# A decoder step on one core: the pairs' elementwise steps and the token sums on VectorE alone, sums begun at the normed prompt, half of the embedding's products later

## The chip, the cores and the metric

The kernel runs as one program on one core of a Trainium2 chip. The metric is the device time of one execution in microseconds (us), as the median of several runs. A profile of one further execution comes with it. Its engines are TensorE (PE, with its weight loads PEld), VectorE (DVE), ScalarE (ACT), GpSimd (POOL) and SyncE (SP, which issues most transfers). The engines run side by side, each in the order of its own queue, and wait for one another by semaphores.

## The reference, cut to what matters

One layer of a hybrid decoder, for a prompt of 512 tokens and for 8 samples of 4 tokens with 4,096 cached positions each; all 544 tokens go through the same weights. After the token mixers it computes, per token:

```
x   = layer_norm(ALPHA * x + mixed, ln1_g, ln1_b)
gate, up = split(x @ w_ffn_up, 2)                 # 1024 -> 2 x 2816
ffn = (silu(gate) * up) @ w_ffn_down
ple = sigmoid(x @ w_ple_gate) * (p @ w_ple)       # p: 256 per token
x   = layer_norm(ALPHA * x + ffn + ple, ln2_g, ln2_b)
```

The change lies between the first of these norms and the product with w_ffn_down. `p @ w_ple` is called the embedding below.

## The kernel before, in words

**Layout.** Activations stand transposed: 128 channels of a block on the partitions, tokens along the free axis (columns 0 to 511 the prompt, 512 to 543 the samples). Full precision is had from three products of parts: a matrix is split into a high part (a copy rounded to the matmul's type) and a low part (the matrix minus its high part), and high x high, high x low and low x high are added up in PSUM (`passes`, L464). The high part is a ScalarE activation or a VectorE copy, the low part an elementwise subtraction (`split`, L275). In the profile wh and wl are a weight unit's parts, x1h and x1l those of the normed x, h of the FFN's hidden rows, th and tl those of the token sums.

**Weights** come in units of 128 x 1024 (512 KB), numbered in the order of use: `GN` (L32) lists the groups and their lengths, `FA` (L29) the units of the first four FFN columns, among which the two units of the embedding stand as "wp". `SRC` (L39) gives each unit's place in memory. `loader` (L372) and `splitter` (L388) fetch and split them ahead of the products.

**The order of the work.** One Python program writes out every engine's queue by hand. `Weave` (L64) plays streams (generators) against a model of the engines' clocks: `wv.t` is TensorE's time, `wv.act`, `wv.dve` and `wv.pool` those of the others; a stream yields a time, a condition or a flag, and the stream of the best priority that may go on goes on. So costs and conditions in the planner decide in which order an engine's instructions stand; the hardware then follows that order and waits where the model was off. Two helpers choose an engine: `tt` (L262) gives a two-input step to GpSimd where the model lets GpSimd finish 0.3 us before VectorE, `evac` (L268) chooses between VectorE and ScalarE. As every instruction is recorded by the engine's wrapper, nearly all VectorE, ScalarE and GpSimd work bears L146, and products L238; the tile names tell them apart.

**From the first norm on.** `norms1` (L1073) norms the prompt in two halves of 256 columns; `norm1` (L1049) scales the residual tiles rr in place, and per group of two channel blocks writes the high part with the bias on ScalarE and the low part with the bias on VectorE. The samples' 32 columns come by a stream of their own, `sample_tail` (L966), which waits for the decode attention, makes its projections and its norm in the tile res, and writes the sample columns of x1h and x1l (L1040). Flags ("x1", part, group) tell what is ready.

**The first four FFN columns** (`NA` = 4, L1421 to L1446) are plain products in two token parts: columns 0 to 255 as soon as the first prompt half is normed, then columns 256 to 543 once the second half and the samples are. In the first part `embed` (L1319) puts four of the embedding's eight output blocks in front of column 1 and four in front of column 2; its results wait in the tiles pw.

**The other 18 FFN columns and the gate of the embedding** go in 22 pairs (`pair`, L497): two weight units and the two token halves are combined as in a 2 x 2 block product with seven instead of eight multiplications. `pair_splits` (L402) forms the four combinations of the weights (s1 = c + d, c = a - c, a = s1 - a, b = b - a; c lies in the tile wq, a and b in wr, s1 in ws) and splits seven operands. `token_sums` (L1375) forms the four combinations of the tokens once, from xw = x1h + x1l, as the tiles tw, and splits them; the flag "tok" lets the pairs begin (L1448). `combine` (L534) adds the seven results up on VectorE, and `act` (L1455, L1490) applies the gate. Behind the 22 pairs `h_parts` (L1475) splits the hidden rows and the products with w_ffn_down begin, two output blocks at a time in the order in which hidden rows come.

**Room.** Large tiles share 39 slots (`slot`, L199); split weights have four buffers of each part.

Of the kernel before, what the change touches and what calls it, by code (L numbers as in the profile page):

```python
# [20 lines left out]
NT = 544  # L21
# [6 lines left out]
EMB = (1, 2)  # L28
FA = []  # L29
for _c in range(NA):  # L30
    FA += [("wp", _w) for _w in range(2) if EMB[_w] == _c] + [("up", 2 * _c), ("up", 2 * _c + 1)]
GN = [("in", 20), ("ga", 8), ("gc", 8), ("ap", 4), ("cp", 4), ("wo", 8), ("wo2", 6),  # L32
      ("fa", len(FA)), ("fb", 2 * NA), ("up", 44 - 2 * NA), ("pg", 8), ("dn", 22)]
# [8 lines left out]
SRC += [BASE["wo2"] + len(FA) + _i for _i in range(NU - BASE["up"])]  # L42
# [133 lines left out]
def step_kernel(ctx: ExitStack, tc: tile.TileContext, xT, pT, ck, cvv, state, pt, W, cv, cc, yT, kT, vT, cvo):  # L176
# [98 lines left out]
    def split(hi, lo, src, *then):  # L275
# [7 lines left out]
        def low():  # L283
            (tt if near else V.tensor_tensor)(out=lo, in0=src, in1=hi.bitcast(F32), op=ALU.subtract)
            flag.update(then)
# [116 lines left out]
    def pair_splits(n):  # L402
# [3 lines left out]
        def put(i, src):  # L406
            sop[n, i] = [big.tile([128, 512], F32R, tag=x, bufs=4, name=x) for x in ("wh", "wl")]
            cur["w"] += 1
            split(*sop[n, i], src, ("so", n, i))
# [14 lines left out]
        tt(out=s1, in0=c, in1=d, op=ALU.add)  # L424
        tt(out=c, in0=a, in1=c, op=ALU.subtract)
        yield done(("so", n, 0))
        tt(out=a, in0=s1, in1=a, op=ALU.subtract)
# [8 lines left out]
        tt(out=b, in0=b, in1=a, op=ALU.subtract)  # L436
# [60 lines left out]
    def pair(n, out):  # L497
# [6 lines left out]
        for i in range(7):  # L504
# [12 lines left out]
            for k in range(4):  # L517
# [3 lines left out]
                for l, (a, b) in enumerate(((w[0], y[0]), (w[0], y[1]), (w[1], y[0]))):  # L521
                    mm(HT * 4.25e-4, o, a[:, c], b, k == 0 and l == 0, k == 3 and l == 2)
# [443 lines left out]
    def sample_tail():  # L966
# [71 lines left out]
        for i, op in ((L1G, ALU.mult), (L1B, ALU.add)):  # L1038
            V.tensor_tensor(out=res, in0=res, in1=cvt[:, i:i + 8].unsqueeze(2).to_broadcast([128, 8, 32]), op=op)
        for g in range(4):  # L1040
# [5 lines left out]
    x1, x1p = [], []  # L1046
    tot1 = []

    def norm1(s, c0, c1, after, tag):  # L1049
# [3 lines left out]
        def each(g):  # L1053
# [8 lines left out]
            for e in range(2):  # L1062
                S.activation(out=h[:, e, c0:c1], in_=x[:, e], func=AF.Identity, bias=bs[e])

            def low():
                for e in range(2):
                    V.scalar_tensor_tensor(out=lo[:, e, c0:c1], in0=x[:, e], scalar=bs[e],
                                           in1=h[:, e, c0:c1].bitcast(F32), op0=ALU.add, op1=ALU.subtract)
                flag.add(("x1", s, g))
            wv.when(on(h), low)  # L1070
        yield from norm(xs, 1.0, c1 - c0, tag, norm_room(), tot1[0][:, c0:c1], each, L1G)

    def norms1():  # L1073
# [4 lines left out]
        rr.clear()  # L1078
# [37 lines left out]
    def main():  # L1116
# [202 lines left out]
        def embed(n, base):  # L1319
            for c in range(len(pw), n):  # L1320
# [4 lines left out]
                                    base + 8 * FA.index(("wp", c // 4)) + 2 * (c % 4))  # L1325
# [49 lines left out]
        def token_sums():  # L1375
            yield lambda: all(("x1", i, g) in flag for i in range(3) for g in range(4))
            x, sums = [], []
            for g in range(4):
                h, lo = (y.bitcast(F32) for y in x1p[g])
                x.append(slot("xw"))  # L1380
                yield pace
                tt(out=x[g], in0=h, in1=lo, op=ALU.add)
            h = lo = None
            for s in range(4):
                sums.append(slot("tw", (128, 4, HT)))
                for g in range(2):
                    l, r = (slice(0, HT), slice(HT, NT))
                    one = x[g + 2 * (s > 0)][:, :, l if s == 3 else r]
                    two = sums[s - 2 if s == 2 else 2][:, 2 * g:2 * g + 2] if s > 1 else x[g][:, :, r if s else l]
                    yield pace  # L1390
                    yield on(one, two)
                    tt(out=sums[s][:, 2 * g:2 * g + 2], in0=one, in1=two, op=ALU.subtract)
                one = two = None
            x.clear()
            for s in (1, 2, 0, 3):
                h, lo = (slot(y, (128, 4, HT), dt=F32R) for y in ("th", "tl"))
                for g in range(2):
                    c = slice(2 * g, 2 * g + 2)
                    yield pace
                    split(h[:, c], lo[:, c], sums[s][:, c], ("ts", s, g))  # L1400
# [14 lines left out]
        def pace():  # L1415
            return wv.dve < wv.t + 1.5
# [4 lines left out]
        for s, (c0, c1) in enumerate(((0, HA), (HA, NT))):  # L1421
            if s:
                ph.clear()
# [23 lines left out]
        p = t = None  # L1447
        yield done("tok")  # L1448
        n = 0
        for c in range(NA, 22):  # L1450
# [4 lines left out]
            def act(x, t, c, n):  # L1455
# [7 lines left out]
                tt(out=g, in0=g, in1=halves(r), op=ALU.mult)  # L1463
# [326 lines left out]
```

## Time and profile before

| | |
|---|---|
| median of 3 runs | 1031.42 us (1030.90 to 1032.55) |
| the profiled execution | 1026.15 us, its span 1024.4 us |
| busy share of the span | TensorE 93%, VectorE 78%, ScalarE 52%, GpSimd 23% |
| granted TensorE clock | 0.98 on average |
| moved | 222 MB, 217 GB/s on average |
| chain that ended last | TensorE 56%, VectorE 27%, DMA 6%, issue 5% |

The page gives the busy time of each engine, the span in 40 slices, the chain of work that ended last, and the costliest groups of instructions. A group or an instruction reads: line, engine, operation, tile written <- tiles read, partitions x elements and type; then the count and the busy time. "[1.40 <-POOL wq L146]" behind an instruction is the time for which its engine was idle before it, and what ended that. In a busy-time row by stretch each engine has its busy time and, in brackets, its instructions. TensorE's products overlap, so the distance between starts tells more of them than their durations.

### The profile page before, as it was taken

What the parts mean: (1) busy time and instruction counts of PE and PEld (TensorE: products, weight loads), DVE (VectorE), ACT (ScalarE), POOL (GpSimd) and SP (SyncE); (2) the same over time, 40 slices, a digit from 0 to 9 for tenths busy, and PEclk for the clock granted to TensorE, in tenths of its full rate; (3) what the DMA queues carried; (4) which work ended last, traced back from release to release, by engine and by line L of the source; (5) the groups of instructions that cost most, each with busy time, mean ns of one, the idle gap of its engine ahead of it and who ended that gap; (6) DMA issues with size and microseconds to landing.
All of it is one profiled execution on the core that took longest, in us unless ns stands there. A gap on an engine that the chain in (4) does not pass through costs nothing.

```text
span 1024.4 us, 22472 instructions
## 1 busy us (share of the span) xinstructions
PE 954.6 (93%) x7978; PEld 827.2 (81%) x7978; DVE 801.8 (78%) x1245; ACT 534.4 (52%) x1040; POOL 233.9 (23%) x202
## 2 busy tenths in 40 slices
PE   7989999999899999999999769999999999999994
PEld 5866667677777986787787769999999998999993
DVE  4798999999857466574986888899999999953375
ACT  4635666567785974343665444444434445621225
POOL 1320322224112002233322550212111112400021
PEclk9999999999999999999999979999999999999998
DMA  9959998999889999999999233322222221222302
GB/s 357 333 165 333 326 315 292 318 334 336 292 305 317 341 346 334 348 339 332 322 324 358 83 103 134 114 83 83 95 112 83 83 98 48 103 83 83 124 1 88
DMA packets 101378, 222.00 MB, mean 217 GB/s; under 512 B 11153, under 2 KB 14482, under 8 KB 101266
## 3 DMA queue, kind: packets, MB, share of 16 engines
q1 hardware_dynamic: 99394, 217.46, 60.6%
q10 hardware_dynamic: 1872, 3.11, 0.8%
q8 instruction: 63, 1.03, 0.4%
q14 instruction: 49, 0.40, 0.1%
HBM read 215.45 MB, written 5.07 MB: 215 GB/s over the span
## 4 chain that ended last, share of the span: by engine, by line
PE 56%; DVE 27%; DMA 6%; issue 5%; ACT 3%; SPq 2%; POOL 1%; ACTq 0%; DVEq 0%; POOLq 0%
PE g L238 38%; PE z L238 6%; PE av L238 6%; DVE wl L146 5%; DVE c L146 4%; DMA kv<-in_ck 2%; PE o L238 2%; DVE pw L146 2%; DVE x L146 2%; DVE pb L146 2%; DVE sg L146 2%; PE tp L238 2%; PE tp L243 1%; DVE wr L146 1%; SPq L228 1%
## 5 line engine op out<-in xcount | busy, mean ns | idle before, releaser
L146 ACT ACTIVATE wh<-wr 128x512 fp32r<-128x512 f32 x236 | 146.5, 626 | 238.8 <-PE g L238 102.0
L146 DVE TENSOR_TENSOR wl<-wr,wh 128x512 fp32r<-128x512 f32 x187 | 130.0, 701 | 50.3 <-ACT wh L146 49.7
L146 POOL TENSOR_TENSOR wl<-wr,wh 128x512 fp32r<-128x512 f32 x53 | 81.8, 1546 | 247.7 <-ACT wh L146 197.3
L238 PE MATMUL g<-xh,wh 128*128 128x272 f32 (+1 forms) x512 | 127.8, 321 | 6.1 <-ACT wh L146 6.1
L238 PE MATMUL g<-h,wh 128*128 128x272 f32 x704 | 123.1, 290 | 1.6 <-DVE h L146 1.6
L238 PE MATMUL g<-xl,wh 128*128 128x272 f32 (+1 forms) x512 | 119.9, 305 | 0.0
L238 PE MATMUL g<-xh,wl 128*128 128x272 f32 (+1 forms) x512 | 119.7, 305 | 0.2 <-POOL wl L146 0.2
L146 DVE SCALAR_TENSOR_TENSOR c<-u,cvt,c 128x512 f32<-128x512 f32 x120 | 109.2, 910 | 3.3
L238 PEld LDWEIGHTS g<-h,wh 128*128 128x128 f32 x704 | 103.2, 189 | 2.7 <-DVE h L146 2.3
L238 PEld LDWEIGHTS g<-xh,wh 128*128 128x128 f32 x512 | 83.2, 191 | 27.0 <-issue 17.5
L238 PEld LDWEIGHTS g<-xh,wl 128*128 128x128 f32 x512 | 83.6, 192 | 4.1 <-POOL wl L146 0.8
L238 PEld LDWEIGHTS g<-xl,wh 128*128 128x128 f32 x512 | 83.7, 191 | 2.6 <-DVE xl L146 0.5
L238 PE MATMUL g<-h,wl 128*128 128x272 f32 x352 | 80.0, 289 | 0.0
L238 PE MATMUL g<-x1h,wh 128*128 128x272 f32 (+2 forms) x216 | 66.1, 306 | 13.8 <-DVE sg L146 12.3
L238 PE MATMUL g<-x1h,wl 128*128 128x272 f32 (+2 forms) x216 | 66.4, 308 | 9.5 <-DVE wl L146 9.2
L238 PE MATMUL z<-kv,qblk 128*32 128x256 f32 x1024 | 65.0, 382 | 2.2 <-DMA kv<-in_ck 2.1
L146 ACT ACTIVATE wh<-wq 128x512 fp32r<-128x512 f32 x87 | 53.8, 620 | 23.4 <-PE g L238 17.9
L146 DVE TENSOR_TENSOR wl<-wq,wh 128x512 fp32r<-128x512 f32 x75 | 56.5, 758 | 10.9 <-ACT wh L146 10.4
L238 PE MATMUL g<-x1l,wh 128*128 128x272 f32 (+2 forms) x216 | 64.7, 299 | 0.0
L238 PE MATMUL av<-kv,dp 128*32 128x512 f32 x512 | 63.6, 613 | 0.0
L146 POOL TENSOR_TENSOR wl<-ws,wh 128x512 fp32r<-128x512 f32 x20 | 26.8, 1341 | 158.1 <-PE g L238 124.1
L146 ACT ACTIVATE pa<-pa 128x384 f32<-128x384 f32 (+1 forms) x96 | 52.5, 555 | 16.8 <-DVE pa L146 15.3
(319 smaller groups left out, 2455.8 us busy)
## 6 DMA issues: line engine op xcount, KB each, us to landing
kv<-in_ck SPq DMA_DIRECT2D x256, 256.0 KB, 4.5
kv<-in_cvv SPq DMA_DIRECT2D x256, 256.0 KB, 5.3
wr<-in_W SPq DMA_DIRECT2D x98, 512.0 KB, 4.3
wq<-in_W SPq DMA_DIRECT2D x37, 512.0 KB, 5.4
wa<-in_W SPq DMA_DIRECT2D x12, 512.0 KB, 9.9
xr<-in_xT SPq DMA_DIRECT2D x8, 272.0 KB, 5.2
out_yT<-pw SPq DMA_DIRECT2D x7, 272.0 KB, 2.3
out_kT<-qk ACTq DMA_DIRECT2D x4, 272.0 KB, 6.0
```

The costliest lines, as they stand in the source:

```text
L146: fn(**kw)
L228: eng.dma_start(out=out, in_=in_)
L238: T.matmul(out, lhsT=lhsT, rhs=rhs, start=start, stop=stop)
L243: T.transpose(out, in_, ident)
```

## The change

Six things change together.

1. `split` takes an engine for the low part; with it, the low part is not given to GpSimd. The pairs' weights, the token sums, the hidden rows and the normed prompt use it; the plain weights do not. The pairs' combinations and the products in `act` are written for VectorE instead of `tt`.
2. In `norm1` the bias is added in place, so that rr holds the normed x, and the parts come from an ordinary `split`.
3. `token_sums` no longer forms xw. It takes its prompt columns from rr as soon as the second prompt half is ready, 240 columns to a half, and the samples' 32 columns later from the tile res, which `sample_tail` hands over in `late_x`; rr is released there.
4. The token sums are split in the order 2, 1, 0, 3, and `pace` lets them go on only while VectorE's clock is less than 0.7 us (before 1.5) ahead of TensorE's.
5. Only the embedding's first unit stays among the first four columns (in front of column 1). The second has a group of its own behind them, and its four output blocks are computed behind the second token part, in front of the wait for "tok".
6. The planner's price of a pair's product is 0.126 us instead of 272 x 4.25e-4 = 0.116 us.

```diff
-EMB = (1, 2)
+EMB = (1,)
...
-      ("fa", len(FA)), ("fb", 2 * NA), ("up", 44 - 2 * NA), ("pg", 8), ("dn", 22)]
+      ("fa", len(FA)), ("fb", 2 * NA), ("wp", 1), ("up", 44 - 2 * NA), ("pg", 8), ("dn", 22)]
...
-    def split(hi, lo, src, *then):
+    def split(hi, lo, src, *then, eng=None):
...
-            (tt if near else V.tensor_tensor)(out=lo, in0=src, in1=hi.bitcast(F32), op=ALU.subtract)
+            (tt if near and eng is None else V.tensor_tensor)(out=lo, in0=src, in1=hi.bitcast(F32), op=ALU.subtract)
...
-            split(*sop[n, i], src, ("so", n, i))
+            split(*sop[n, i], src, ("so", n, i), eng=V)
...
-        tt(out=s1, in0=c, in1=d, op=ALU.add)
-        tt(out=c, in0=a, in1=c, op=ALU.subtract)
+        V.tensor_tensor(out=s1, in0=c, in1=d, op=ALU.add)
+        V.tensor_tensor(out=c, in0=a, in1=c, op=ALU.subtract)
         yield done(("so", n, 0))
-        tt(out=a, in0=s1, in1=a, op=ALU.subtract)
+        V.tensor_tensor(out=a, in0=s1, in1=a, op=ALU.subtract)
...
-        tt(out=b, in0=b, in1=a, op=ALU.subtract)
+        V.tensor_tensor(out=b, in0=b, in1=a, op=ALU.subtract)
...
-                    mm(HT * 4.25e-4, o, a[:, c], b, k == 0 and l == 0, k == 3 and l == 2)
+                    mm(0.126, o, a[:, c], b, k == 0 and l == 0, k == 3 and l == 2)
...
+        late_x.append(res)
         for g in range(4):
             yield lambda: len(x1p) > g
...
             for e in range(2):
-                S.activation(out=h[:, e, c0:c1], in_=x[:, e], func=AF.Identity, bias=bs[e])
-
-            def low():
-                for e in range(2):
-                    V.scalar_tensor_tensor(out=lo[:, e, c0:c1], in0=x[:, e], scalar=bs[e],
-                                           in1=h[:, e, c0:c1].bitcast(F32), op0=ALU.add, op1=ALU.subtract)
-                flag.add(("x1", s, g))
-            wv.when(on(h), low)
+                S.activation(out=x[:, e], in_=x[:, e], func=AF.Identity, bias=bs[e])
+            split(h[:, :, c0:c1], lo[:, :, c0:c1], x, ("x1", s, g), eng=V)
...
         def token_sums():
-            yield lambda: all(("x1", i, g) in flag for i in range(3) for g in range(4))
-            x, sums = [], []
-            for g in range(4):
-                h, lo = (y.bitcast(F32) for y in x1p[g])
-                x.append(slot("xw"))
-                yield pace
-                tt(out=x[g], in0=h, in1=lo, op=ALU.add)
-            h = lo = None
+
+            sums = []
+            yield lambda: all(("x1", 1, g) in flag for g in range(4))
             for s in range(4):
                 sums.append(slot("tw", (128, 4, HT)))
                 for g in range(2):
-                    l, r = (slice(0, HT), slice(HT, NT))
-                    one = x[g + 2 * (s > 0)][:, :, l if s == 3 else r]
-                    two = sums[s - 2 if s == 2 else 2][:, 2 * g:2 * g + 2] if s > 1 else x[g][:, :, r if s else l]
+                    d = sums[s][:, 2 * g:2 * g + 2, :240]
+                    one = rr[g + 2 * (s > 0)][:, :, 0:240] if s == 3 else rr[g + 2 * (s > 0)][:, :, HT:512]
+                    two = rr[g][:, :, HT:512] if s else rr[g][:, :, 0:240]
+                    if s > 1:
+                        two = sums[s - 2 if s == 2 else 2][:, 2 * g:2 * g + 2, :240]
                     yield pace
                     yield on(one, two)
-                    tt(out=sums[s][:, 2 * g:2 * g + 2], in0=one, in1=two, op=ALU.subtract)
-                one = two = None
-            x.clear()
-            for s in (1, 2, 0, 3):
+                    V.tensor_tensor(out=d, in0=one, in1=two, op=ALU.subtract)
+            yield lambda: all(("x1", 2, g) in flag for g in range(4))
+            res = late_x.pop()
+            yield on(res)
+            t1, t3, t2, t4 = (t[:, :, 240:] for t in sums)
+            for g in range(2):
+                c = slice(2 * g, 2 * g + 2)
+                V.tensor_tensor(out=t1[:, c], in0=res[:, c], in1=rr[g][:, :, 240:HT], op=ALU.subtract)
+            V.tensor_tensor(out=t3, in0=res[:, 4:8], in1=res[:, 0:4], op=ALU.subtract)
+            V.tensor_tensor(out=t2, in0=res[:, 4:8], in1=t1, op=ALU.subtract)
+            for g in range(2):
+                c = slice(2 * g, 2 * g + 2)
+                V.tensor_tensor(out=t4[:, c], in0=rr[2 + g][:, :, 240:HT], in1=t2[:, c], op=ALU.subtract)
+            one = two = d = res = t1 = t2 = t3 = t4 = None
+            rr.clear()
+            for s in (2, 1, 0, 3):
...
-                    split(h[:, c], lo[:, c], sums[s][:, c], ("ts", s, g))
+                    split(h[:, c], lo[:, c], sums[s][:, c], ("ts", s, g), eng=V)
...
-            return wv.dve < wv.t + 1.5
+            return wv.dve < wv.t + 0.7
...
                 if s == 0:
-                    yield from embed(4 * sum(e <= c for e in EMB), base)
+                    if c in EMB:
+                        yield from embed(4, base + 8 * FA.index(("wp", 0)))
                     h_tile()
...
         p = t = None
+        base = cur["next"]
+        cur["next"] += 8
+        yield from embed(8, base)
+        ph.clear()
         yield done("tok")
...
-                tt(out=g, in0=g, in1=halves(r), op=ALU.mult)
+                V.tensor_tensor(out=g, in0=g, in1=halves(r), op=ALU.mult)
...
-                split(*hs[c], h_raw[c], ("hh", c))
+                split(*hs[c], h_raw[c], ("hh", c), eng=V)
```

The other products of the two `act` functions change from `tt` to `V.tensor_tensor` in the same way.

More of the change, by code (lines that the diff above doesn't have):

```diff
@@ L27 @@
 NA = 4
-EMB = (1, 2)
+EMB = (1,)
 FA = []
 for _c in range(NA):
-    FA += [("wp", _w) for _w in range(2) if EMB[_w] == _c] + [("up", 2 * _c), ("up", 2 * _c + 1)]
+    FA += [("wp", _w) for _w in range(len(EMB)) if EMB[_w] == _c] + [("up", 2 * _c), ("up", 2 * _c + 1)]
 GN = [("in", 20), ("ga", 8), ("gc", 8), ("ap", 4), ("cp", 4), ("wo", 8), ("wo2", 6),
-      ("fa", len(FA)), ("fb", 2 * NA), ("up", 44 - 2 * NA), ("pg", 8), ("dn", 22)]
+      ("fa", len(FA)), ("fb", 2 * NA), ("wp", 1), ("up", 44 - 2 * NA), ("pg", 8), ("dn", 22)]
 BASE, NU = {}, 0
@@ L41 @@
 SRC += [BASE["wo2"] + FA.index(("up", _i)) for _i in range(2 * NA)]
-SRC += [BASE["wo2"] + len(FA) + _i for _i in range(NU - BASE["up"])]
+SRC += [BASE["wo2"] + len(FA) + _i for _i in range(NU - BASE["wp"])]
 PAIRS = [(BASE["up"] + 2 * _i, BASE["up"] + 2 * _i + 1) for _i in range(22 - NA)]
@@ L1043, in sample_tail @@
             split(h[:, :, 512:544], lo[:, :, 512:544], res[:, 2 * g:2 * g + 2], ("x1", 2, g))
-    x1, x1p = [], []
+    x1, x1p, late_x = [], [], []
     tot1 = []
@@ L1077, in norms1 @@
         r_t.clear()
-        rr.clear()
     def first_sample(xr, wq):
@@ L1324, in embed @@
                 yield from products(p, [(s, a, b) for s, (a, b) in enumerate(FULL)], 2, lambda k: ph[k],
-                                    base + 8 * FA.index(("wp", c // 4)) + 2 * (c % 4))
+                                    base + 2 * (c % 4))
                 if c % 2 == 0:
@@ L1422, in main @@
             if s:
-                ph.clear()
                 yield lambda: all(("x1", i, g) in flag for i in (1, 2) for g in range(4))
@@ L1466, in act @@
                 yield on(t, x)
-                tt(out=halves(h_raw[c]), in0=g, in1=t, op=ALU.mult)
+                V.tensor_tensor(out=halves(h_raw[c]), in0=g, in1=t, op=ALU.mult)
                 drop()
@@ L1495, in act @@
                 yield on(x)
-                tt(out=halves(pw[c]), in0=halves(pw[c]), in1=g, op=ALU.mult)
+                V.tensor_tensor(out=halves(pw[c]), in0=halves(pw[c]), in1=g, op=ALU.mult)
                 yield done(("sum", n, 6))
@@ L1500, in act @@
                 yield on(t)
-                tt(out=halves(pw[c + 1]), in0=halves(pw[c + 1]), in1=t, op=ALU.mult)
+                V.tensor_tensor(out=halves(pw[c + 1]), in0=halves(pw[c + 1]), in1=t, op=ALU.mult)
                 drop()
@@ L1728, in layout @@
     wu = {"up": np.stack([ug, uu], axis=1).reshape(44, 128, 1024), "wp": _units(d["w_ple"][0])}
-    W += [wu[n][i:i + 1] for n, i in FA] + [wu["up"][2 * NA:]]
+    W += [wu[n][i:i + 1] for n, i in FA] + [wu["wp"][1:], wu["up"][2 * NA:]]
     dn = _units(d["w_ffn_down"][0]).reshape(22, 128, 8, 128).transpose(0, 2, 1, 3).reshape(176, 128, 128)
```

## The prediction

> **What bounds the kernel now.** I read the page's first part, then busy time by stage from the first products with the normed prompt on, then in the slow stages the chain of waits and VectorE's and GpSimd's instructions in order of time.
>
> ```profile
> PE 954.6 (93%) x7978; PEld 827.2 (81%) x7978; DVE 801.8 (78%) x1245; ACT 534.4 (52%) x1040; POOL 233.9 (23%) x202
> ```
>
> TensorE is busy 93% of the span, so an edit that adds no products can win at most what TensorE waits. By stage (columns: TensorE, weight loads, VectorE, ScalarE, GpSimd, granted clock, DMA share, GB/s):
>
> ```profile
> 577.50:622.00 44.50, 31.86 (x193) 30.95 (x194) 38.88 (x46) 19.83 (x41) 23.65 (x14) 0.81 0.35 123
> 655.50:826.20 170.70, 162.58 (x1262) 159.29 (x1261) 158.39 (x248) 73.86 (x135) 30.21 (x23) 1.00 0.26 93
> 871.20:900.00 28.80, 27.16 (x210) 26.46 (x210) 28.70 (x33) 16.24 (x29) 12.79 (x8) 1.00 0.25 89
> ```
>
> The reader is to see two leaks: 44.50 - 31.86 = 12.6 us in 577 to 622, where the second token half of the first four FFN columns runs, at a clock of 0.81, and 170.70 - 162.58 = 8.1 us in a stretch of the pairs, with VectorE nearly full in both. What the pairs lose stands in the chain of waits, by the start of the products into the PSUM tile g, once a pair:
>
> ```profile
> 634.12 3.02 PE g L238 x24
> ...
> 644.69 3.02 PE g L238 x24
> ```
>
> ```profile
> 667.11 3.03 PE g L238 x22
> ...
> 678.17 3.05 PE g L238 x22
> ...
> 826.20 3.04 PE g L238 x22
> ```
>
> Their ends are the first products of the first pair, in the same chain, and the first products with the hidden parts:
>
> ```profile
> 622.04 1.51 PE z L238 x12
> ```
>
> ```profile
> 870.15 0.66 PE L238 MATMUL g<-h,wh 128*128 128x272 f32 x4
> ```
>
> From 634.12 to 644.69 a pair takes 10.57 us with TensorE never idle: that is TensorE's floor, 84 products of 0.126. The 14 pairs from 667.11 to 826.20 take 159.09 / 14 = 11.36 each, the one from 667.11 takes 11.06, so its neighbour some 11.7. All 22 run from 622.04 to 870.15: 248.1 us, 15.6 over 22 x 10.57 = 232.5. Why, VectorE and GpSimd show:
>
> ```profile
> 652.09 0.69 DVE L146 TENSOR_TENSOR ws<-wq 128x512 f32<-128x512 f32 x1
> 652.81 0.69 DVE L146 TENSOR_TENSOR wq<-wr,wq 128x512 f32<-128x512 f32 x1
> ```
>
> ```profile
> 657.28 1.66 DVE L146 TENSOR_TENSOR wr<-wr 128x512 f32<-128x512 f32 x1
> 658.87 0.71 DVE L146 TENSOR_TENSOR x<-x,r 128x544 f32<-128x544 f32 x1
> 659.62 0.72 DVE L146 TENSOR_TENSOR hr<-x,sg 128x544 f32<-128x544 f32 x1
> 660.26 0.69 DVE L146 TENSOR_TENSOR wl<-wr,wh 128x512 fp32r<-128x512 f32 x1
> 660.86 0.72 DVE L146 TENSOR_TENSOR x<-g,sg 128x544 f32<-128x544 f32 x1
> 661.50 0.68 DVE L146 TENSOR_TENSOR wl<-wq,wh 128x512 fp32r<-128x512 f32 x1
> 662.09 0.43 DVE L146 TENSOR_TENSOR x<-z,x 128x272 f32<-128x272 f32 x1
> 662.44 0.68 DVE L146 TENSOR_TENSOR wl<-wr,wh 128x512 fp32r<-128x512 f32 x1
> 663.04 0.69 DVE L146 TENSOR_TENSOR ws<-wq 128x512 f32<-128x512 f32 x1
> 665.13 0.69 DVE L146 TENSOR_TENSOR wr<-ws,wr 128x512 f32<-128x512 f32 x1 [1.40 <-POOL wq L146]
> 665.74 0.72 DVE L146 TENSOR_TENSOR sg<-tp,x 128x544 f32<-128x544 f32 x1
> ```
>
> ```profile
> 657.11 1.29 POOL L146 TENSOR_TENSOR wl<-ws,wh 128x512 fp32r<-128x512 f32 x1 [9.66 <-PE g L238]
> 663.81 1.29 POOL L146 TENSOR_TENSOR wq<-wr,wq 128x512 f32<-128x512 f32 x1 [5.41 <-DVE ws L146]
> ```
>
> GpSimd takes one low half (wl<-ws) in each pair and one subtraction (wq<-wr,wq) in every second. The subtraction holds VectorE up for 1.40. The low half overlaps VectorE's wr<-wr, which then takes 1.66 where a step of the same size takes 0.69: it starts just behind GpSimd's and ends as if it had waited for it. So help from GpSimd costs VectorE more than it saves.
>
> **The change, part by part.** *Pairs on VectorE alone.* The time from the start of one step to the start of the next is its price while the queue is full: a low half 0.60 (660.26 to 660.86), the addition ws 0.72, the steps on wr 0.61 (665.13 to 665.74), 544 elements 0.64 (659.62 to 660.26), 272 elements 0.35 (662.09 to 662.44), the gate's first product 0.75 (658.87 to 659.62). A pair has seven low halves (4.20), two steps of 0.72 and two of 0.61 (2.66), five combining steps (0.64 + 0.35 + 0.64 + 0.35 + 0.35 = 2.33) and the two products of the gate (0.75 + 0.64 = 1.39): 10.58. That is level with TensorE's 10.57, so neither has room and small misses add up; I take 10.65. 22 x 10.65 = 234.3, a gain of 13.8. Bounds: 15.6 (TensorE's floor), and 4.8 if all pairs run at 11.06, the present pair without the subtraction on GpSimd. The planner's new 0.126 per product is what the trace has; it costs nothing by itself.
>
> [...]
>
> *Token sums.* They run now behind the sample's last norm:
>
> ```profile
> L146 DVE TENSOR_TENSOR xw<-x1h,x1l 128x1088 f32<-128x1088 f32 x4 | 6.3, 1605 | 0.0
> L146 DVE TENSOR_TENSOR tw<-xw 128x544 f32<-128x544 f32 x4 | 5.9, 1524 | 0.0
> L146 DVE TENSOR_TENSOR tl<-tw,th 128x544 fp32r<-128x544 f32 x5 | 5.4, 1144 | 0.0
> L146 DVE TENSOR_TENSOR tw<-xw,tw 128x544 f32<-128x544 f32 x3 | 5.4, 1814 | 0.0
> ```
>
> ```profile
> 549.20:577.50 28.30, 16.24 (x35) 1.00 0.57 210
> ```
>
> The four xw (6.3) go, since the normed x is kept in place. The eight sums shrink to 480 columns (about 0.57 each by the rows above, 4.6) and run ahead of the sample: VectorE is idle for 28.30 - 16.24 = 12.1 us between 549 and 577, which hides them. If that cover were gone they would push the sample's norm back by up to 4.6. Seven small steps for the sample's 32 columns come behind it, an estimate of 0.25 each from the 272-element row, under 2 us. Of the 38.9 us that VectorE works in 577 to 622, 6.3 + 5.9 + 5.4 = 17.6 go; the small steps (1.7), the three of the eight low halves tl that are not in VectorE's row and so run on GpSimd (1.9), and the moved embedding's two splits and copies (some 2.5) come: 27.4.
>
> *Half of the embedding's products.* 48 products of 0.126 = 6.05 us leave the stretch before the sample is ready and come behind the first columns.
>
> ```profile
> 575.78 0.28 PE L238 MATMUL g<-x1h,wl 128*128 128x256 f32 x1
> 577.59 0.37 PE L238 MATMUL g<-x1h,wh 128*128 128x288 f32 x1 [1.54 <-ACT x1h L146]
> ```
>
> ```profile
> 607.07 0.61 PE L238 MATMUL g<-x1h,wh 128*128 128x288 f32 x1 [4.68 <-DVE sg L146]
> ```
>
> ```profile
> 605.00:610.00 5.00, 2.93 (x12) 2.93 (x13) 3.44 (x8) 0.45 (x1) 0.00 (x0) 0.50 0.40 128
> ```
>
> TensorE would be through with the first half at 575.8 - 6.05 = 569.8 and then wait for the sample until 577.6, which its own chain sets. So the moved products are a cost of 6.05 ahead, and they pay only if TensorE would wait behind. The idle 7.7 us also costs clock: behind the wait of 4.68 the granted clock was 0.50 for 5 us, worth 2.5, and with its way back I take 3.2.
>
> [...]
>
> *This stage's sum.* 192 products of 288 columns, at 0.126 x 288 / 272 = 0.133, are 25.6 us. With VectorE at 27.4 us of work beside some 37, of the 12.6 us of waits I keep 2. The pairs then begin at 577.6 + 25.6 + 3.2 + 2 + 6.05 = 614.5 instead of 622.04: a gain of 7.6. Bounds: 12.8 (no clock lost, no wait), and -6.05 (the columns still end at 622 and the embedding comes on top).
>
> *The norm's rewrite.* Each group of the normed prompt gets one more ScalarE split and one VectorE low half instead of two steps.
>
> ```profile
> 514.36 0.87 DVE L146 SCALAR_TENSOR_TENSOR x1l<-rr,cvt,x1h 128x256 fp32r<-128x256 f32 x2
> ```
>
> ```profile
> 519.80 0.28 PE L238 MATMUL g<-x1h,wh 128*128 128x256 f32 x1
> ```
>
> The first half is split by 515.2 and first used at 519.80: a later split of about 0.7 a group hides in those 4.6 us, if the groups stay pipelined, and the second half has until 577. Cost 0, up to 2 if ScalarE falls behind.
>
> *Tail.* A few steps of the last pairs and of the split of the hidden rows go from GpSimd to VectorE; each costs 0.64 and saves a step held up by about 1.0. VectorE sets that stretch (28.70 of 28.80), TensorE waits 1.6 there, and I leave it so, give or take 2.
>
> **Sum.** 7.6 + 13.8 = 21.4. The profiled execution took 1026.15 us (span 1024.4), so it would take 1004.8; the median of the runs is 1031.42, 5.3 above it, and 1031.4 - 21.4 = 1010.0.
>
> **The rivals.** (1) Pairs limited by VectorE at 11.06: 4.8 + 7.6 = 12.4, 1019. For it: both engines level, four buffers of split weights between them; against it: the pair from 634.12 ran at TensorE's floor. (2) The first columns stay bound by VectorE: GpSimd keeps some ten steps there (weights' low halves, the gates) that can hold VectorE up by 1 us each, 27.4 + 10 = 37, the whole stage. Then the embedding comes on top: 13.8 - 6.05 = 7.8, 1023.7. (3) Everything fits: 12.8 + 15.6 = 28.4, 1003. (4) The change does not do what it says, because the slots that the early sums need come free only when the sample's weights are used, so that they run where they ran: the embedding is then lost and the pairs still gain, near (2). (5) Slower: VectorE's steps do not overlap once it is alone. By durations a pair is 7 x 0.68 + 4 x 0.69 + 0.72 + 0.43 + 0.72 + 0.43 + 0.43 + 0.71 + 0.72 = 11.7, with the gaps of dependent steps 11.8; 22 x 11.8 = 259.6 is 11.5 over 248.1, less 7.6 of the front: 1035. It decides from (248.1 + 7.6) / 22 = 11.62 a pair. Against it: the starts 0.60 apart under load.
>
> **How the numbers follow.** My forecast 0.54, (1) 0.18, (2) and (4) together 0.09, (3) 0.14, (5) 0.05. The forecast's own bounds are 1005 to 1016. A range from 1001 to 1020 takes in (1) and (3) and leaves out (2), (4) and (5), 14 in 100, and some strays at its ends. About 0.2%, 2 us, is what a measurement of this kernel can tell from no change. Faster by over that is all but (5) and a corner of (2): 0.93; within it 0.02; slower 0.05.
>
> **What would show it.** GpSimd empty between the first pair and the last; VectorE's 512-element steps all near 0.69, none at 1.7; starts of g 10.6 to 10.7 apart, 22 pairs in 233 to 236 us; the first pair near 614; sums tw at 550 to 565; TensorE idle ahead of the sample by 6 to 8 us; the embedding's second products right before the pairs. Wrong would be a cadence at 11 or more, a first pair at 622 or later, a sample norm later than 578, or new waits of TensorE behind 870.

## The result, and the profile after

The kernel after takes 997.63 us (median of 4 runs, 994.74 to 999.53); the kernel before, run beside it, takes 1031.16 us (4 runs, 1028.96 to 1032.55). The ratio is 0.9674 (95% interval 0.9641 to 0.9708), a gain of 33.5 us. The forecast of 1010.0 had the direction and 21.4 of the 33.5; the range that it gave ended at 1001, 3.4 us above the measured time. The profiled execution of the kernel after took 999.53 us with a span of 997.7, so 1.8 us lie outside the span, as before.

The first line of the page of the kernel after, busy times and shares of the span:

```profile
PE 949.2 (95%) x7978; PEld 827.7 (83%) x7978; DVE 782.6 (78%) x1286; ACT 543.6 (54%) x1044; POOL 182.6 (18%) x159
```

Its busy time by stage, in the columns that the prediction explained: the first columns behind the samples, as long a stretch of the pairs as was shown of before, and 29 us at the start of the tail.

```profile
577.65:613.50 35.85, 34.54 (x242) 33.56 (x243) 25.10 (x51) 19.70 (x38) 10.32 (x5) 0.95 0.44 148
646.80:817.50 170.70, 170.70 (x1358) 170.70 (x1358) 169.12 (x291) 85.66 (x147) 0.00 (x0) 1.00 0.28 100
847.00:876.00 29.00, 29.00 (x231) 29.00 (x230) 27.65 (x39) 16.97 (x29) 11.88 (x5) 1.00 0.24 84
```

TensorE's waits have all but gone in the three stretches: its idle time falls from 12.6 to 1.3 us in the first row, and from 8.1 and 1.6 to nothing in the others. VectorE is full in the pairs (169.12 of 170.70), but TensorE no longer waits for it, and GpSimd is empty there. One wait has grown: just ahead of the first row TensorE waits 4.80 us for the samples, where it waited 1.54 before. The chain that ended last, at the first pair, at two neighbouring pairs, at a late one and at the end of the pairs (start, duration):

```profile
613.53 1.52 PE z L238 x12
...
636.20 3.02 PE g L238 x24
...
646.77 3.02 PE g L238 x24
...
837.09 3.02 PE g L238 x24
...
846.15 102.55 PE g L238 x810
```

From 636.20 to 646.77 is 10.57 us, and from 646.77 to 837.09 are 18 pairs at 10.573: the whole stage runs at the distance that only single pairs had. The last line is the tail beginning: 810 products in 102.55 us without a gap.

VectorE in one pair of the kernel after, in order of time; between the lines left out stand steps of the same kinds:

```profile
711.23 0.69 DVE L146 TENSOR_TENSOR wr<-wr 128x512 f32<-128x512 f32 x1
711.83 0.69 DVE L146 TENSOR_TENSOR wl<-ws,wh 128x512 fp32r<-128x512 f32 x1
712.43 0.72 DVE L146 TENSOR_TENSOR hr<-x,sg 128x544 f32<-128x544 f32 x1
...
715.98 0.69 DVE L146 TENSOR_TENSOR ws<-wq 128x512 f32<-128x512 f32 x1
716.70 0.69 DVE L146 TENSOR_TENSOR wq<-wr,wq 128x512 f32<-128x512 f32 x1
717.43 0.69 DVE L146 TENSOR_TENSOR wr<-ws,wr 128x512 f32<-128x512 f32 x1
...
721.17 0.72 DVE L146 TENSOR_TENSOR x<-x,r 128x544 f32<-128x544 f32 x1
721.80 0.68 DVE L146 TENSOR_TENSOR wr<-wr 128x512 f32<-128x512 f32 x1
```

No step takes 1.7 any more, low halves start 0.60 apart, and from wr<-wr to the next wr<-wr are 721.80 - 711.23 = 10.57: TensorE's pace.

Where the time went is read from five points that every trace has: A, the first product with the normed prompt; S, the first product of 288 columns (the samples are there); B, the first product of a pair; C, the first product with the hidden parts; and D, the span's end. All in us, from one profile each, every cell rounded by itself:

| kernel | A to S | S to B | B to C | C to D | A to D |
|---|---|---|---|---|---|
| before | 57.8 | 44.3 | 248.3 | 154.2 | 504.6 |
| after | 56.5 | 35.7 | 232.6 | 151.8 | 476.6 |

From A on the change is worth 28.0: 9.8 up to the first pair, 15.7 in the pairs, 2.5 in the tail. The other 5.5 us of the 33.5 are not found behind A. Up to the first norm, 16 us before A, the two kernels' instruction queues are the same on every engine; the section on the prediction comes back to the stretch between there and A, and to what is left.

### The profile page after: what moved, and what is told of

Read it like the earlier page. It is cut to its first block, busy times and chain, and to the rows that moved or that the text cites. A ratio compares the mean times of both kernels' runs of the same rounds, so it can differ in the third digit from the quotient of the medians.

```text
span 997.7 us, 22430 instructions
## 1 busy us (share of the span) xinstructions
PE 949.2 (95%) x7978; PEld 827.7 (83%) x7978; DVE 782.6 (78%) x1286; ACT 543.6 (54%) x1044; POOL 182.6 (18%) x159
## 4 chain that ended last, share of the span: by engine, by line
PE 74%; DVE 11%; DMA 8%; ACT 3%; issue 2%; SPq 1%; ACTq 0%; POOL 0%; DVEq 0%; POOLq 0%
PE g L238 44%; PE z L238 10%; PE av L238 9%; PE o L238 6%; PE tp L238 5%; DVE c L146 3%; DMA kv<-in_ck 2%; DMA kv<-in_cvv 2%; PE tp L243 2%; DVE pb L146 1%; DMA wr<-in_W 1%; DMA wa<-in_W 1%; DVE wl L146 1%; ACT pa L146 1%; DVE dl L146 1%
## 5 line engine op out<-in xcount | busy, mean ns | idle before, releaser
L146 DVE TENSOR_TENSOR wl<-wr,wh 128x512 fp32r<-128x512 f32 x190 | 132.2, 700 | 52.2 <-ACT wh L146 51.2
L146 DVE SCALAR_TENSOR_TENSOR c<-u,cvt,c 128x512 f32<-128x512 f32 x120 | 113.7, 947 | 3.3
L238 PE MATMUL g<-x1h,wl 128*128 128x272 f32 (+2 forms) x216 | 63.3, 293 | 0.0
L238 PEld LDWEIGHTS g<-h,wl 128*128 128x128 f32 x352 | 58.0, 188 | 0.0
```

Source lines behind the costliest of these rows:

```text
L146: fn(**kw)
L238: T.matmul(out, lhsT=lhsT, rhs=rhs, start=start, stop=stop)
```

## The experiments

The same distances for every experiment, with the medians of its timed runs and its ratio to the kernel before on the same chip:

| kernel | A to S | S to B | B to C | C to D | A to D | median | ratio (95%) |
|---|---|---|---|---|---|---|---|
| b0_again | 57.8 | 44.2 | 248.2 | 154.3 | 504.5 | 1030.49 | 1.0013 (0.9994 to 1.0031) |
| e1_pairs | 57.8 | 44.1 | 233.4 | 159.9 | 495.2 | 1021.65 | 0.9919 (0.9889 to 0.9949) |
| e2_sums | 61.4 | 32.3 | 248.6 | 154.2 | 496.5 | 1015.98 | 0.9863 (0.9841 to 0.9884) |
| e3_embed_back | 59.9 | 32.3 | 232.6 | 151.8 | 476.6 | 998.82 | 0.9709 (0.9686 to 0.9732) |
| after_again | 56.8 | 35.6 | 232.6 | 151.8 | 476.7 | 996.20 | 0.9680 (0.9652 to 0.9707) |
| e4_low_on_gpsimd | 55.9 | 35.8 | 244.1 | 151.8 | 487.6 | 1010.29 | 0.9824 (0.9799 to 0.9849) |
| e5_sub_on_gpsimd | 56.9 | 35.6 | 237.0 | 152.0 | 481.5 | 1003.62 | 0.9755 (0.9724 to 0.9786) |
| e6_old_price | 56.0 | 35.7 | 233.8 | 153.2 | 478.6 | 1001.93 | 0.9730 (0.9705 to 0.9756) |
| e9_embed_alone | 60.2 | 49.0 | 248.4 | 154.2 | 511.8 | 1036.04 | 1.0073 (1.0044 to 1.0103) |
| e7_plain_lows | 54.8 | 37.0 | 232.6 | 151.8 | 476.2 | 996.67 | 0.9695 (0.9658 to 0.9733) |
| e10_lows_embed_back | 55.9 | 30.7 | 232.6 | 151.8 | 470.9 | 991.02 | 0.9640 (0.9612 to 0.9667) |
| e11_all_on_vectore | 53.8 | 35.0 | 232.6 | 151.8 | 473.2 | 995.65 | 0.9675 (0.9637 to 0.9712) |

The experiments ran on four chips. The medians of the kernel before on them were 1028.26 (b0 to e3), 1028.78 (after_again to e6), 1029.75 (e9, e7, e10) and 1029.47 (e11).

**The kernel before once more.** No edit.

> The kernel before, unchanged, with a second profile. Theory (small terms and a basis): the change is worth 26.7 us in the two profiled spans, 8.5 in the stage of the first FFN columns, 15.5 in the pairs and 2.7 behind them; the rest of the 33 us between the medians is that the first profiled execution of the kernel before was short by some 5 us. Then this profile's span lies near 1028 to 1030, and the difference to the first lies in waits ahead of 500 us, where the change touches nothing. Rival (hidden effect): the span is again near 1024, and the change does something in timed runs that profiled ones do not show.

Its profiled execution took 4.8 us longer (span 1029.2 against 1024.4), and all of that lies ahead of A: 524.7 against 519.8, with 504.5 from A on. So what lies ahead scatters by some 5 from one execution to the next, while from A on this kernel repeats to 0.1 us. The kernel after repeats less well in one place: its two profiles and those of e4, e5 and e6, whose queues are the same up to the first pair, have 55.9 to 56.9 from A to S. There a difference of 1 us in A to S, and so in A to D, shows nothing; the other distances repeat to some 0.2.

**The pairs alone.** The kernel before, with the low halves of the pairs' weights, the pairs' combinations and the products in `act` on VectorE:

```diff
-            split(*sop[n, i], src, ("so", n, i))
+            split(*sop[n, i], src, ("so", n, i), eng=V)
...
-        tt(out=s1, in0=c, in1=d, op=ALU.add)
+        V.tensor_tensor(out=s1, in0=c, in1=d, op=ALU.add)
```

> The kernel before with the pairs' elementwise steps on VectorE alone; sums, norm, embedding and planner's price as before. Theory (GpSimd's steps hold VectorE up): 22 pairs at 10.57 to 10.65 us, 232.6 to 234.3 between the first pair and the products with the hidden parts, so 14 to 16 us faster than before, and up to 1 more behind the pairs. Rival (the planner's price matters): with 0.116 us a product the planner orders VectorE's steps worse, the pairs stay at 10.8 to 11.06, 5 to 10 us faster.

The pairs gain 14.9, as the theory had it, but the tail loses 5.7, where the theory allowed 1. GpSimd in the tail of this kernel:

```profile
872.79 14.09 POOL L146 TENSOR_TENSOR wl<-wr,wh 128x512 fp32r<-128x512 f32 x1 [7.27 <-ACT wh L146]
```

What ended TensorE's waits between 870 and 900 (us in total, times, longest):

```profile
PE g L238 <- POOL wl L146: 5.1, 1, 5.1
```

One low half that takes 1.29 elsewhere (at 898.80 in the same kernel) took 14.09, while VectorE ran steps with two inputs back to back (a start every 0.60 to 0.64 us from 872.47 to 885.04); TensorE waited 5.1 for it, and the granted clock was 0.66 on average from 885 to 895. Here GpSimd's step did not only hold VectorE up: it was itself starved.

**The sums alone.** The kernel before with parts 2 to 4 of the change (norm in place, early sums, order and pace) and nothing else:

```diff
+            S.activation(out=x[:, e], in_=x[:, e], func=AF.Identity, bias=bs[e])
+            split(h[:, :, c0:c1], lo[:, :, c0:c1], x, ("x1", s, g), eng=V)
...
+            yield lambda: all(("x1", 1, g) in flag for g in range(4))
```

> The kernel before with only the norm in place and the early token sums (their low halves on VectorE); pairs and embedding as before. Theory (the sums alone make the front's gain, the embedding's move adds nothing): the first pair begins 10 to 14 us sooner than before, as TensorE is busy with the embedding while it waits for the sample; 9 to 13 us faster. Rival (the embedding has to cover the end of the sums): the first pair begins at most 5 us sooner, with TensorE waiting for the sums, 3 to 5 us faster.

A to B falls by 102.1 - 93.8 = 8.3: the samples come 3.6 later, and what follows takes 11.9 less. That lies between the theory's 10 to 14 and the rival's 5. The stretch of the first columns was indeed held by VectorE's sums, but the later samples give a part of the gain back.

**The embedding back.** The kernel after, with all four output blocks of the embedding's second half in front of column 2 again:

```diff
-EMB = (1,)
+EMB = (1, 2)
...
-        yield from embed(8, base)
```

> The changed kernel with the second half of the embedding's products back in front of the third of the first columns. Theory (the move costs what TensorE then waits ahead of the sample): TensorE's wait of some 6 us before 578 closes, the first pair begins 3 to 6 us sooner, 3 to 6 us faster than the changed kernel. Rival (the move pays behind): the first pair waits for the sums' parts or for VectorE, the same time or up to 4 us slower than the changed kernel.

A to D is 476.6, that of the kernel after; the time is the rival's. Against the theory, the wait ahead of the samples does not close: they come 3.3 later (A to S 59.9 for 56.5), TensorE still waits 3.33, and what follows is 3.4 shorter. TensorE at S and at the next long wait of this kernel:

```profile
580.17 0.58 PE L238 MATMUL g<-x1h,wh 128*128 128x288 f32 x1 [3.33 <-ACT th L146]
...
588.48 0.40 PE L238 MATMUL g<-x1h,wh 128*128 128x288 f32 x1 [3.61 <-DVE sg L146]
```

VectorE ahead of the samples there:

```profile
569.34 2.32 DVE L146 TENSOR_TENSOR tw<-rr,tw 128x480 f32<-128x480 f32 x2
571.58 1.76 DVE L146 TENSOR_TENSOR wl<-wr,wh 128x512 fp32r<-128x512 f32 x1
```

GpSimd at the same time, and behind the samples:

```profile
569.09 1.48 POOL L146 TENSOR_TENSOR wl<-wr,wh 128x512 fp32r<-128x512 f32 x1 [0.55 <-ACT wh L146]
571.50 1.29 POOL L146 TENSOR_TENSOR wl<-wr,wh 128x512 fp32r<-128x512 f32 x1 [0.93 <-ACT wh L146]
...
581.44 5.40 POOL L146 TENSOR_TENSOR wl<-wr,wh 128x512 fp32r<-128x512 f32 x1 [3.73 <-issue]
```

VectorE's steps at 569.34 and 571.58 take about 1.1 too long each, where GpSimd's started just ahead of them, and at 581.44 GpSimd is the one that is starved. That the samples come later with the embedding in front may therefore be GpSimd's doing; e7 and e10 below test that.

**The kernel after once more.** No edit.

> The changed kernel, unchanged, timed again beside the kernel before on one chip. In the six profiles so far the first product with the normed prompt starts between 519.4 and 524.7 us, and from there the kernel before takes 504.5 and 504.6, the changed one 476.6. Theory (the change is worth 28 us, what lies ahead of the first norm scatters): the medians differ by 27 to 30 us, a ratio of 0.971 to 0.974, and the profile shows again 476 to 477 from the first product with the normed prompt to the end. Rival (the change also shortens what lies ahead): the difference stays at 33, a ratio of 0.967 to 0.968, with the first such product at 516 to 519.

A to D is 476.7, so the 28 us from A on stand. The ratio of the medians, 0.9680, is the rival's: the gain is again larger than these 28 us explain (28.0 of 1028.78 would be 0.9728, outside the interval). But A stood at 525.2 in this profile, not at the rival's 516 to 519, so the 5 us don't show in a profile as an earlier A.

**One low half on GpSimd in each pair.** The kernel after, with the low half of s1 given to GpSimd:

```diff
-            split(*sop[n, i], src, ("so", n, i), eng=V)
+            split(*sop[n, i], src, ("so", n, i), eng=G if i == 4 else V)
```

> The changed kernel with one low half in each pair (that of s1) given to GpSimd. Theory (GpSimd's step gets in while VectorE reads PSUM and then holds up a step with two operands in SBUF by its whole length): VectorE saves 0.60 and loses 1.0 to 1.1 a pair, 11.06 a pair, the pairs 10 to 11 us longer than 232.6. Rival (VectorE is merely relieved): the pairs stay at 232.6, the same time.

The pairs take 11.5 us more, 0.52 a pair, a little over the theory's 10 to 11, though VectorE has a step less. GpSimd and VectorE in one pair:

```profile
703.37 1.35 POOL L146 TENSOR_TENSOR wl<-ws,wh 128x512 fp32r<-128x512 f32 x1 [9.83 <-PE g L238]
```

```profile
702.88 0.69 DVE L146 TENSOR_TENSOR wl<-wq,wh 128x512 fp32r<-128x512 f32 x1
703.48 1.82 DVE L146 TENSOR_TENSOR x<-x,r 128x544 f32<-128x544 f32 x1
705.22 0.68 DVE L146 TENSOR_TENSOR wr<-wr 128x512 f32<-128x512 f32 x1
```

The gate's first product starts 0.11 behind GpSimd's step, and its successor starts 1.74 later instead of 0.63: the 0.60 saved costs 1.11. The theory's "while VectorE reads PSUM" is not what this pair shows: GpSimd's step starts 0.20 before the end of wl<-wq,wh, which reads no PSUM tile. In the kernel before, 10 of GpSimd's 20 low halves of s1 started during a VectorE step that reads the PSUM tile z or av, and 10 near the end of another step; in all 20 VectorE's next step took 1.66 to 1.81. It is so all along: 21 of VectorE's steps in the 22 pairs take over 1.5 us, where the longest in the kernel after takes 0.73. Nearly three quarters of the pairs' gain is gone with one step a pair.

**One subtraction on GpSimd in every second pair.**

```diff
-        V.tensor_tensor(out=c, in0=a, in1=c, op=ALU.subtract)
+        (G if n % 2 else V).tensor_tensor(out=c, in0=a, in1=c, op=ALU.subtract)
```

> The changed kernel with the subtraction c = a - c given to GpSimd in every second pair. Theory (a step of 1.3 us in a chain of VectorE's steps is waited for): VectorE idles 1.4 us for it where the step itself took 0.72, so 0.6 to 0.7 more in every second pair, 6 to 8 us in all. Rival (it is hidden, as the weights are split ahead of the products): the same time within 1 us.

The pairs take 4.3 more, less than the theory's 6 to 8, but far from the rival's nothing. The two engines around it:

```profile
706.61 1.29 POOL L146 TENSOR_TENSOR wq<-wr,wq 128x512 f32<-128x512 f32 x1 [20.25 <-DVE ws L146]
```

```profile
705.85 0.69 DVE L146 TENSOR_TENSOR ws<-wq 128x512 f32<-128x512 f32 x1
707.94 0.69 DVE L146 TENSOR_TENSOR wr<-ws,wr 128x512 f32<-128x512 f32 x1 [1.40 <-POOL wq L146]
```

From ws to wr it is 2.09 here and 717.43 - 715.98 = 1.45 in the kernel after, 0.64 more for one step less; a pair with it takes 0.4 more (4.3 / 11). The rest fits the room that VectorE has, 170.70 - 169.12 = 1.6 us in 16 pairs, 0.2 in two.

**The planner's old price.**

```diff
-                    mm(0.126, o, a[:, c], b, k == 0 and l == 0, k == 3 and l == 2)
+                    mm(HT * 4.25e-4, o, a[:, c], b, k == 0 and l == 0, k == 3 and l == 2)
```

> The changed kernel with the planner's old price of a pair's product, 0.116 us. The kernel with only the pairs' steps moved had its pairs in 233.4 us but took 8 us longer behind them, with one low half of GpSimd of 14.1 us among VectorE's steps and TensorE waiting 5.1 us for it. Theory A (the old price makes that order): behind the pairs some 160 us, 6 to 9 us slower than the changed kernel. Theory B (it came from hidden rows that could still go to GpSimd by the planner): behind the pairs 151.7 as in the changed kernel, the same time within 2 us.

The pairs take 1.2 more and the tail 1.4: the price by itself is worth some 2.6 us of the order of work, which the forecast had put at nothing. Theory A falls, as the tail is 153.2 and not 160; the 2.6 are a little over theory B's 2. That the tail of e1 came from hidden rows on GpSimd, as B has it, is not shown by a run of its own.

**The embedding's move alone,** in the kernel before:

```diff
-EMB = (1, 2)
+EMB = (1,)
...
+        yield from embed(8, base)
```

> The kernel before with only the embedding's second half moved behind the first FFN columns; sums, norm, pairs as before. Theory (behind the sample VectorE sets the stretch in the kernel before, not TensorE, so 6.05 us of products put there lie in part beside VectorE's work, but nothing is won ahead either, where the sample sets the time): first product with the normed prompt to first pair 102 to 108 us (before 102.1), of it 55 to 58 to the first 288-column product (before 57.8) and 45 to 50 behind it (before 44.3); to the span's end 504 to 511 (before 504.5). Rival (the embedding in front holds the sample's chain back by some 3 us in any kernel, so that moving it is a gain by itself, and the shorter wait keeps the clock up): under 100 us to the first pair, 500 to 502 to the end.

It costs 7.2 us (A to D 511.8), a little over both the theory's upper end and the 6.05 of the products themselves. The samples are not earlier but 2.4 later. VectorE in front of the samples' last steps, y_s:

```profile
579.94 0.42 DVE L146 TENSOR_TENSOR sg<-g,sg 128x256 f32<-128x256 f32 x1 [1.54 <-ACT sg L146]
580.28 0.71 DVE L146 TENSOR_TENSOR y_s<-y_s 128x32 f32<-128x32 f32 x1
```

They stand in VectorE's queue behind a gate step that waits 1.54 for ScalarE, which is the larger part of the 2.4. The rival, that the embedding in front holds the samples back in any kernel, falls.

**The plain weights' low halves on VectorE,** on top of the kernel after:

```diff
-            split(*hl[u, e], halved(raw[u])[e], ("w", u, e))
+            split(*hl[u, e], halved(raw[u])[e], ("w", u, e), eng=V if u >= BASE["fa"] else None)
```

> The kernel after, and in addition the low halves of the plain weights, from the first FFN columns on, on VectorE alone, so that GpSimd has next to none of them. Theory (from the sample on TensorE is the limit in pairs and tail, so what GpSimd still does there costs nothing): first product with the normed prompt to the span's end 475.5 to 478 us (after 476.6), the tail 151 to 152.5. Rival (GpSimd's remaining low halves still hold VectorE up by about 1 us each in the first columns and cost TensorE there): 472 to 475, all of the gain between the first 288-column product and the first pair (after 35.8, down to 32 to 34).

As the theory had it: 476.2 against 476.6. The samples come 1.7 earlier, but TensorE has nothing left to do by then and waits 5.53 for them, and what follows takes 1.3 more.

**Both: these low halves on VectorE and the embedding back.** The two edits of e3 and e7 together.

> The kernel after with both: the plain weights' low halves on VectorE and the embedding's second half back in front of column 2. Theory (each is worth nothing): first product with the normed prompt to the span's end 475.5 to 478.5 us (after 476.6). Rival (VectorE free of GpSimd brings the sample's norm earlier again, which is what the embedding in front had cost): 472 to 475, with the first 288-column product at most 57.5 us behind the first product with the normed prompt (59.9 with the embedding alone put back).

The theory that each is worth nothing falls, and the gain passes the rival's: A to D 470.9, 5.7 less than the kernel after. TensorE at S:

```profile
573.09 0.40 PE L238 MATMUL g<-x1h,wh 128*128 128x288 f32 x1 [0.35 <-ACT sg L146]
```

Now the embedding fills the wait ahead (0.35 is left of it) and the samples stay on time (55.9, against 59.9 with GpSimd at work), so S to B is shorter by 37.0 - 30.7 = 6.3, the embedding's products. This kernel is the fastest of all: 991.02 us, 0.9640 of before, where e7 on the same chip has 996.67. So with these low halves on VectorE the change's move of the embedding costs 476.2 - 470.9 = 5.3 us, and in the kernel after the low halves on GpSimd covered that up. Their move also changes the order of VectorE's queue; how much of the 5.3 is GpSimd's holding VectorE up and how much is the order, these runs don't separate.

**Everything on VectorE.** On top of e10, every `tt` from the normed prompt to the end of the pairs:

```diff
-        e = G if end("pool", (2 * n + 100) / 960, in0, in1) + GBIAS < end("dve", (n + 66) / 960, in0, in1) else V
+        clear = ("x1", 0, 0) in flag and ("h", 21, 1) not in flag
+        e = G if not clear and end("pool", (2 * n + 100) / 960, in0, in1) + GBIAS < end("dve", (n + 66) / 960, in0, in1) else V
```

> The kernel with the plain weights' low halves on VectorE and the embedding back, and in addition the gates of the first FFN columns, and the samples' last two-input steps beside them, on VectorE too, so that GpSimd does nothing from the normed prompt to the end of the pairs. Theory (what GpSimd still had there, one gate step of 5.48 us above all, cost TensorE some 2.4 us of waits and a lower clock behind the sample): first 288-column product to first pair 27 to 29.5 us (30.7 without this edit), first product with the normed prompt to the span's end 467.5 to 470 us (470.9 without). Rival (VectorE is then full there and the steps land on the path of the sample's norm): 470.5 to 474.

The theory falls: A to D is 473.2, 2.3 more than e10. The rival has the time, but not the path: the samples come 2.1 earlier, and TensorE waits behind them:

```profile
587.75 0.61 PE L238 MATMUL g<-x1h,wh 128*128 128x288 f32 x1 [6.06 <-DVE sg L146]
```

VectorE ahead of that sg step:

```profile
582.22 2.63 DVE L146 TENSOR_TENSOR tl<-tw,th 128x544 fp32r<-128x544 f32 x4
584.77 0.69 DVE L146 TENSOR_TENSOR wl<-wr,wh 128x512 fp32r<-128x512 f32 x1
585.37 1.36 DVE L146 TENSOR_TENSOR tl<-tw,th 128x544 fp32r<-128x544 f32 x2
586.64 0.69 DVE L146 TENSOR_TENSOR wl<-wr,wh 128x512 fp32r<-128x512 f32 x1
587.24 0.95 DVE L146 TENSOR_TENSOR sg<-g,sg 128x288 f32<-128x288 f32 x2
```

The step that frees TensorE's PSUM tile stands behind six of the token sums' low halves, which nobody needs before the pairs begin at 608.8. VectorE is the limit here, busy 13.89 of the 13.96 us from S to that product, and the order of its queue decides; whether another order would keep both gains wasn't tried.

## Why the prediction was right and where it was wrong

**Right: the mechanism.** The pairs were slow because GpSimd's steps hold VectorE up, by their length (e4: 1.82 for a step that takes 0.72 alone, beside GpSimd's 1.35) or by being waited for (e5: 1.40). e1 shows it from the one side (pairs 14.9 faster with no other part of the change), e4 and e5 from the other (11.5 and 4.3 slower with one step given back).

**Mis-sized: the pairs, 13.8 forecast, 15.7 measured.** The failed step is "That is level with TensorE's 10.57, so neither has room and small misses add up; I take 10.65". It took 10.573 (232.6 / 22). VectorE had more room than was counted: the gate's first product was charged 0.75 from a stretch with GpSimd in it and takes 0.63 (721.17 to 721.80), and the price of 0.126, "costs nothing by itself", orders the work better by 1.2 us (e6). Rival (3) had this term right.

**Mis-sized: the front, 7.6 forecast, 9.8 measured.** Sums ahead of the samples, and VectorE's work of 27.4 beside some 37, came true as 25.10 of 35.85. The samples were about 1 us earlier than the forecast took them to be (A to S 55.9 to 56.9 for 57.8), and the clock cost less than "with its way back I take 3.2". TensorE waited 4.80 at S, not 7.7; ahead of S stand other waits (7.2 us from A to S in all, before 5.2) and a granted clock at half from 550.8 to 557.6, which before had not. Of the products behind S

```profile
577.65 0.40 PE L238 MATMUL g<-x1h,wh 128*128 128x288 f32 x1 [4.80 <-ACT x1h L146]
...
579.43 0.44 PE L238 MATMUL g<-x1h,wh 128*128 128x288 f32 x1
579.67 0.44 PE L238 MATMUL g<-x1l,wh 128*128 128x288 f32 x1
```

some 14, from 578 to 581.4, stood 0.24 apart instead of 0.133, at a granted clock of 0.51: 14 x 0.107 = 1.5 us, about half of the 3.2.

**Right in sign, for a part only: the embedding.** That "the moved products are a cost of 6.05 ahead" is what e9 (7.2) and the pair of e7 and e10 (5.3) show. In the kernel after itself (e3) the move is worth nothing, which the forecast's steps would not have given: they left out that, with low halves on GpSimd, the samples' norm comes later when the embedding is in front (59.9, against 55.9 in e10).

**Missed: the tail, 0 forecast, 2.5 measured.** The step "VectorE sets that stretch, TensorE waits 1.6 there, and I leave it so" failed: TensorE has no gap in the 102.55 us from 846.15 on. 1.4 of it comes with the planner's price (e6). It is just beyond the 2 that the forecast allowed.

**Put at nothing: the norm's rewrite, 0 forecast, 1.9 measured.** The step is "Cost 0, up to 2 if ScalarE falls behind", and what it gave lies ahead of A. From the last step that ScalarE's queue has in common in the two kernels, the split of a weight at 502.86 (at 506.03 in the kernel after), to A it is 16.94 us before and 15.07 after. All ten profiles with the norm in place have 15.05 to 15.20 there; e1, without it, has 16.94, and b0_again and e9 have 18.53. e2 has it with parts 2 to 4 alone, of which only the norm's rewrite acts there. The rows point to the mechanism of the pairs once more. VectorE, GpSimd and TensorE in the kernel before:

```profile
508.30 2.35 DVE L146 TENSOR_TENSOR wl<-wq,wh 128x512 fp32r<-128x512 f32 x2
508.05 1.44 POOL L146 TENSOR_TENSOR wl<-wq,wh 128x512 fp32r<-128x512 f32 x1
510.10 0.39 PE L238 MATMUL g<-m,wl 128*128 128x256 f32 x1 [2.29 <-DVE wl L146]
```

and VectorE and TensorE in the kernel after, where GpSimd has its low half only at 514.80:

```profile
510.75 1.29 DVE L146 TENSOR_TENSOR wl<-wq,wh 128x512 fp32r<-128x512 f32 x2
511.49 0.39 PE L238 MATMUL g<-m,wl 128*128 128x256 f32 x1 [0.64 <-DVE wl L146]
```

Two low halves took 2.35 behind GpSimd's and take 1.29 without it, and TensorE's wait for them falls from 2.29 to 0.64.

**Open: what is left, 1 to 4 us ahead of that.** The terms put right give 28.0 + 1.9 = 29.9 and 1031.4 - 29.9 = 1001.5, still inside the range. In b0_again the wait of 2.29 was followed by half the clock (0.50 from 514 to 515), and with the 18.53 of b0_again and e9 the sum is 31.5, the time 999.9. The rest is between medians, not between profiles. For each timed kernel, the difference of its median from before's less the difference of the two distances from A to D is a number that no edit behind A explains. For the kernel after it is 5.5 and 4.7; for the others with the norm in place it runs from 0.9 (e6) to 5.0 (e10), and for the three without it is -2.8 (e1), -2.3 (the kernel before against itself) and 0.9 (e9). So a part of it goes with the norm's rewrite, 1.9 or 3.5 by the profiles. What remains follows no one part of the change, and A moves by more from profile to profile (517.2 to 525.2). Its cause stays open. The failed step is "A range from 1001 to 1020 takes in (1) and (3)": its lower end lies 2 us below rival (3), which counts no gain from the norm and the tail. These two gave 1.9 + 2.5 = 4.4, and the range had nothing for the stretch ahead, where two runs of one kernel differ by 5.

**Fallen: rival (5).** With VectorE alone in the pairs, steps lasting 0.69 still start 0.60 apart in a full queue (711.23, 711.83 and 712.43 above).

## What to carry to other kernels

Before giving GpSimd a share of VectorE's elementwise work, add VectorE's steps by their start-to-start distance alone: if they fit under the engine that should be the limit, GpSimd's help can be a loss. Here each step of 512 elements given away in the pairs saved VectorE 0.60 and cost it about 1.1 (e4). Where VectorE itself was the limit (the first columns in e11) the same rule did not pay (A to D 473.2, against 470.9 in e10), and there the order of its queue counted. The work that was moved out of a wait into a full stretch cost nearly its whole length (5.3 of 6.05 between e7 and e10), and whether the wait exists should be judged in the kernel with all other edits in.

## What the runs showed of the hardware

**Either engine held the other up.** A GpSimd step that takes 1.29 alone took 14.09 in e1, and 6.25 in the kernel after. GpSimd there, and VectorE at its first pause:

```profile
871.02 6.25 POOL L146 TENSOR_TENSOR wl<-wr,wh 128x512 fp32r<-128x512 f32 x1 [7.58 <-ACT wh L146]
```

```profile
876.99 0.83 DVE L146 TENSOR_TENSOR wl<-wr,wh 128x512 fp32r<-128x512 f32 x1 [0.87 <-ACT wh L146]
```

VectorE ran steps with two inputs without a gap from 871.02 until that pause began at 876.1, and GpSimd's step ended at 877.27, about its own length later. So GpSimd held VectorE up by one step of its own, about 1.1 us in e3 and e4, and VectorE held GpSimd up for some 5 us here and 13 in e1, while its own run of such steps lasted.

**Half the clock behind a wait of 2 us, but not each time.** TensorE in e10, around a short wait:

```profile
579.11 0.40 PE L238 MATMUL g<-x1h,wh 128*128 128x288 f32 x1 [2.00 <-DVE sg L146]
...
580.00 0.29 PE L238 MATMUL g<-x1h,wh 128*128 128x288 f32 x1
...
581.04 0.45 PE L238 MATMUL g<-x1h,wl 128*128 128x288 f32 x1
581.28 0.45 PE L238 MATMUL g<-x1h,wh 128*128 128x288 f32 x1
```

The first products behind it came at full pace; then, a microsecond after the work had resumed, the granted clock was at half from about 580.2 to 583.6. In e3 it fell at about 589.9, also for some 3.4 us, behind a wait of 3.61 that had ended at 588.48. But the same wait was not always followed by it. The kernel before has the wait of 2.29, shown above, in each of its two profiles, ending at 510.10 in the first and at 513.38 in b0_again. One microsecond of TensorE behind it, in the first and in b0_again (busy time and products, granted clock, DMA share, GB/s):

```profile
511.00:512.00 1.00, 1.00 (x10) 1.00 1.03 332
```

```profile
514.00:515.00 1.00, 1.00 (x9) 0.50 1.07 397
```

The stretch from the last common step to A is 1.6 us longer in b0_again (18.53 for 16.94), and so it is in e9; e1 has the 16.94 of the first profile. What decides between the two clocks, these runs don't show.
